# Rotary scores over 128 rows with a zero-padded key, and a forgetting bias built on VectorE from sums broadcast through DRAM

## The chip, the cores and the metric

The kernel runs on one core of one Trainium2 chip. The metric is the device time of one execution in microseconds (us). TensorE (PE in the profile, PEld for its weight loads), VectorE (DVE), ScalarE (ACT) and GpSimd (POOL) each work through an instruction queue of their own in a fixed order; SyncE (SP) and GpSimd issue transfers.

## The reference

Two layers of a transformer trunk on 256 tokens of width 2048, in float32. Each layer normalises and modulates its input, projects it, and runs three attention branches of 8 heads with 128 columns each. The branches' outputs are gated, projected, merged by sigmoid gates and projected once more. The change touches the scores of two branches. Queries are taken in two blocks of 128; the first sees 128 keys, the second 256.

```python
# latent attention: per head 128 plain columns and 64 rotary ones; the rotary key is the same for all heads
k_a = jnp.concatenate([kv_a[..., :MLA_NOPE], k_pe], axis=-1)
s = jnp.einsum('bqhd,bkhd->bhqk', q, k) / math.sqrt(MLA_NOPE + MLA_ROPE)

# forgetting attention: a bias from running sums of log-sigmoids, per head
log_f = jax.nn.log_sigmoid(f_logit + fox_bias)
fcum = jnp.transpose(jnp.cumsum(log_f, axis=1), (0, 2, 1))
s = jnp.einsum('bqhd,bkhd->bhqk', q, k) / math.sqrt(HEAD_DIM)
s = s + fcum[:, :, q0:q0 + n_q, None] - fcum[:, :, None, :n_k]
p = jax.nn.softmax(jnp.where(mask, s, NEG_INF), axis=-1)
```

The third branch, stick-breaking attention, has plain 128-row scores and is not changed.

## The kernel before

**Weight products.** Nearly all of TensorE's time goes into products of activations with weights. Weights come from DRAM in units of 256 rows by up to 1024 columns (`weight_unit`, line 222) into four buffers `raw`. Each unit is split in two halves of 128 rows, and each half into a rounded part `whi` (ScalarE, line 235) and its remainder `wlo` (VectorE, line 237), four buffers each. Three matmuls of 512 columns per pair and output bank follow (lines 281 to 283). So VectorE and ScalarE have to deliver one split half for every 12 matmuls.

**What sets the order.** The program is recorded with a scheduling layer that places each engine's instructions by its own estimate of when they are ready. It sets the attention instructions in between the matmuls of whatever product comes next (mostly the merge gate, `merge_gate`, line 485). On the chip each queue then runs in that order, and a waiting instruction holds up all that stand behind it.

**Latent attention** (line 726). Transposed plain queries and keys lie in `qT` and `kT`, 128 rows a head. The rotary queries of two heads share one 128-row block of `peT`: head 2i in rows 0 to 63, head 2i+1 in rows 64 to 127. The rotary key `kpT` holds the same 64 rows twice, one above the other. `scores` (line 459) does for each query block a plain matmul over 128 rows and adds a rotary one over 64 rows, of the upper or the lower half. In float32 each of these matmuls is a pair of instructions in the trace (x2).

**Forgetting attention** (line 731). The logits `flog` are early results. Line 750 sums them over tokens with a triangle of ones; the sums, plain and negated, are split into rounded and remainder rows (lines 752 to 761). For each head, line 764 selects that head's rows on VectorE, and `biased_scores` (line 468) puts the bias into the score bank by a 256-column matmul (line 472) and adds the plain scores (line 473).

**Softmax** (`attention_head`, line 423). VectorE adds the mask and takes the row maximum in one instruction per query block (line 428), ScalarE does the exponential (line 434), TensorE transposes the result (line 442), ScalarE copies it (line 444), TensorE multiplies with the values (lines 447 to 449), and VectorE scales and gates the output (line 455). Scores, transposes and outputs take turns in two PSUM buffers (`att_tile`).

**Background work.** In both layers weights of the modulation vectors are summed on VectorE (line 300) in between. GpSimd adds them across partitions (line 327) and writes one result to DRAM (line 330), which is broadcast later to all partitions (line 837). In layer 1 this sum across partitions falls just ahead of the forgetting attention (line 723).

Of the kernel before, what the change touches and what calls it, by code (L numbers as in the profile page):

```python
# [9 lines left out]
F32 = mybir.dt.float32  # L10
F32R = mybir.dt.float32r
I32 = mybir.dt.int32
AF = mybir.ActivationFunctionType
ALU = mybir.AluOpType

P = 128
# [26 lines left out]
def trunk(  # L43
# [82 lines left out]
    # quad[:, q] marks rows 32q..32q+7; columns 4 and 5 the last two and the first two such groups  # L126
    quad = const.tile([P, 6], F32, name="quad")
    nc.gpsimd.memset(quad, 0.0)
    for q in range(4):
        nc.gpsimd.memset(quad[32 * q:32 * q + H, q:q + 1], 1.0)  # L130
        nc.gpsimd.memset(quad[32 * q:32 * q + H, 4 + (q < 2):5 + (q < 2)], 1.0)
    sel = const.tile([P, H], F32, name="sel")
    nc.vector.tensor_tensor(out=sel, in0=ident[:, :H], in1=ident[:, 32:32 + H], op=ALU.add)
    for q in (2, 3):
        nc.vector.tensor_tensor(out=sel, in0=sel, in1=ident[:, 32 * q:32 * q + H], op=ALU.add)
# [50 lines left out]
    def rsqrt(v, eps, scale=1.0):  # L186
        """1 / sqrt(scale * v + eps): seed from the exponent bits, three Newton steps."""
# [55 lines left out]
    class Gemm:  # L243
        """out[token, parts' columns] = act^T @ parts, in banks of at most 512 columns."""
# [110 lines left out]
    def normalise_row(src, dst, t, mean):  # L355
        """dst = (src - mean) / sqrt(var + eps) of one token tile; dst is scratch until then."""
# [46 lines left out]
    def rope(src, dst, t, n, eng):  # L403
        """src, dst: [P, n, 2, 32]"""
# [7 lines left out]
    def rms_rows(src, n, t):  # L412
        """src [P, n] in SBUF, scaled in place by its reciprocal root mean square."""
# [8 lines left out]

    def attention_head(S, mask, scale, h, v, g):
        sm = tmp.tile([P, 3 * P], F32, tag="sm", name="sm")
        mx = small.tile([P, 2], F32, tag="mx", name="mx")
        segs = ((0, P), (P, 3 * P))
        for t, (a, b) in enumerate(segs):
            nc.vector.tensor_tensor_reduce(
                out=sm[:, a:b], in0=S[t], in1=mask[:, 2 * P - (b - a):], scale=1.0, scalar=-3.0e38,
                op0=ALU.add, op1=ALU.max, accum_out=mx[:, t:t + 1])  # L430
# [37 lines left out]
    def biased_scores(qT, kT, h, bl, br):  # L468
        S = att_tile()
        for t, n in enumerate((P, 2 * P)):  # L470
            ts_, a = slice(t * P, (t + 1) * P), t * SEQ
            nc.tensor.matmul(S[:, a:a + SEQ], bl[:, ts_], br, start=True, stop=False)
            nc.tensor.matmul(S[:, a:a + n], qT[:, h, ts_], kT[:, h, :n], start=False, stop=True)
        return S[:, :P], S[:, SEQ:]

# [15 lines left out]
    for l in range(DEPTH):  # L491
# [6 lines left out]
        # ================= branch a: latent attention =================  # L498
# [4 lines left out]
        peT = big.tile([P, H // 2 + 1, SEQ], F32, tag="sig", name="peT")  # L503
        qpT, kpT = peT[:, :H // 2], peT[:, H // 2]
# [4 lines left out]
        def evac_a0(t, h, ps):  # L509
# [8 lines left out]
            else:  # L518
# [11 lines left out]
                nc.vector.tensor_copy(out=kpT[:, t * P:(t + 1) * P], in_=tp[:, 2 * P:3 * P])  # L530
# [173 lines left out]
        for n in range(3):  # L704
# [21 lines left out]
            if n == 0:  # L726
                for h in range(H):
                    pb = slice(64 * (h % 2), 64 * (h % 2) + 64)
                    S = scores(qT, kT, h, [(qpT[pb, h // 2], kpT[pb])])
                    attention_head((S[:, :P], S[:, P:3 * P]), m_mla, 1.0 / math.sqrt(HD + ROPE), h, v, g)  # L730
            elif n == 1:
# [7 lines left out]
                # rows 0.., 32.., 64.., 96..: head sums of lf up to a token, twice plain and twice negated  # L739
                lf4 = tmp.tile([P, NT, 4, 32], F32, tag="sm", name="lf4")  # L740
                nc.vector.memset(lf4, 0.0)
                nc.vector.tensor_scalar(
                    lf4[:, :, :2, :H], lf.rearrange("p t (g h) -> p t g h", g=1).broadcast_to([P, NT, 2, H]),
                    root, None, op0=ALU.mult)
                nc.vector.tensor_scalar(
                    lf4[:, :, 2:, :H], lf.rearrange("p t (g h) -> p t g h", g=1).broadcast_to([P, NT, 2, H]),
                    -root, None, op0=ALU.mult)
                ps = att_tile()
                l4 = lf4.rearrange("p t g h -> p t (g h)")
                nc.tensor.matmul(ps[:, :SEQ], l4[:, 0], tri, start=True, stop=False)  # L750
                nc.tensor.matmul(ps[:, P:SEQ], l4[:, 1], tri[:, :P], start=False, stop=True)
                fr = big.tile([P, 4, SEQ], F32R, tag="yhi", name="fr")
                fh, bl = fr[:, 0], fr[:, 1]
                fw = big.tile([P, 3, SEQ], F32, tag="ylo", name="fw")
                fl, base = fw[:, 0], fw[:, 1]
                split(ps[:, :SEQ], fh, fl)
                for dst, q in ((bl, 0), (base, 2)):
# [159 lines left out]
```

## Time and profile before

| | us |
|---|---|
| median of 3 runs | 2192.75 (2189.21 to 2192.93) |
| span of the profiled execution | 2188.8 |
| TensorE busy | 2087.3 (95%) |
| VectorE busy | 1453.2 (66%) |
| ScalarE busy | 985.9 (45%) |
| GpSimd busy | 63.7 (3%) |

For the profiled execution the page gives the span, from its first to its last instruction, and no other time. The median of the runs lies 3.95 us above it, the fastest 0.41 us. The ends of matmuls are modelled and overlap the next one's start, so the pace of TensorE is read from starts: the distance between the starts of two rows.

### The profile page before, as it was taken

Reading aid. Unit: us, or ns where it says so; the run is one execution under the profiler, and the core shown is the slowest. Engines: PE = TensorE matmul, PEld = TensorE weight load, DVE = VectorE, ACT = ScalarE, POOL = GpSimd, SP = SyncE. Lnnn points to the kernel's source line nnn. Section 1 sums busy time; section 2 is a strip of 40 time slices with the busy share of each in tenths; the row PEclk is TensorE's granted clock in tenths of the full one; section 3 lists DMA queues with packets and bytes.
Section 4 is the critical chain, followed back from the end, with each engine's and each line's share of the span. In section 5 each row is a group of like instructions: output and inputs, shape, how many; then the busy total and the mean of one; then the engine's idle time right before and its main releaser. Section 6 shows DMA issues by size and latency. Waiting matters only on the chain.

```text
span 2188.8 us, 24876 instructions
## 1 busy us (share of the span) xinstructions
PE 2087.3 (95%) x9630; PEld 1704.1 (78%) x9630; DVE 1453.2 (66%) x1944; ACT 985.9 (45%) x1259; POOL 63.7 (3%) x80
## 2 busy tenths in 40 slices
PE   4999999999999999999969999999989999999996
PEld 2877878887888878787848878888868888878885
DVE  6898845677558777888586755555575554466466
ACT  4435644343453445634355644444444444464442
POOL 0000000002000020002000000000020000000000
PEclk8999999999999999999979999999999999999998
DMA  8996635787548867786635736666645555555652
GB/s 312 343 333 234 192 116 173 271 300 268 181 152 295 314 257 253 290 323 212 210 135 177 233 121 221 233 221 220 234 160 172 192 183 184 193 190 200 192 204 96
DMA packets 137781, 481.03 MB, mean 220 GB/s; under 512 B 14656, under 2 KB 18880, under 8 KB 127424
## 3 DMA queue, kind: packets, MB, share of 16 engines
q1 hardware_dynamic: 133296, 464.69, 61.3%
q0 software_dynamic: 2080, 14.70, 1.7%
q8 instruction: 75, 1.23, 0.2%
q10 hardware_dynamic: 2288, 0.07, 0.1%
q14 instruction: 42, 0.34, 0.0%
HBM read 475.21 MB, written 4.21 MB: 219 GB/s over the span
## 4 chain that ended last, share of the span: by engine, by line
PE 87%; DVE 8%; ACT 3%; issue 2%; DMA 1%; POOL 0%; DVEq 0%; SPq 0%; POOLq 0%; ACTq 0%
PE acc L282 25%; PE acc L283 25%; PE acc L281 25%; DVE wlo L237 2%; PE att L464 2%; PE acc L620 2%; PE acc L621 2%; PE acc L619 1%; ACT whi L235 1%; PE att L481 1%; PE att L447 1%; PE att L442 1%; PE att L399 1%; DVE wlo L611 1%; DVE cum L782 1%
## 5 line engine op out<-in xcount | busy, mean ns | idle before, releaser
L237 DVE TENSOR_TENSOR wlo<-raw,whi 128x1024 fp32r<-128x1024 f32 (+2 forms) x648 | 813.7, 1261 | 572.9 <-ACT whi L235 572.7
L235 ACT ACTIVATE whi<-raw 128x1024 fp32r<-128x1024 f32 (+2 forms) x648 | 677.6, 1051 | 834.6 <-PE acc L283 782.7
L282 PE MATMUL acc<-wlo,uhi 128*128 128x512 f32 (+1 forms) x1856 | 733.2, 395 | 12.2 <-DVE wlo L237 12.2
L281 PE MATMUL acc<-whi,uhi 128*128 128x512 f32 (+1 forms) x1856 | 727.7, 394 | 4.0 <-ACT whi L235 3.9
L283 PE MATMUL acc<-whi,ulo 128*128 128x512 f32 (+1 forms) x1856 | 727.9, 392 | 0.0
L282 PEld LDWEIGHTS acc<-wlo,uhi 128*128 128x128 f32 x1856 | 351.3, 189 | 82.9 <-DVE wlo L237 14.2
L281 PEld LDWEIGHTS acc<-whi,uhi 128*128 128x128 f32 x1856 | 350.1, 189 | 76.1 <-ACT whi L235 4.3
L283 PEld LDWEIGHTS acc<-whi,ulo 128*128 128x128 f32 x1856 | 350.9, 189 | 68.5 <-issue 1.3
L282 PE MATMUL acc<-wlo,yhi 128*128 128x512 f32 x384 | 149.5, 389 | 2.0 <-DVE wlo L237 2.0
L281 PE MATMUL acc<-whi,yhi 128*128 128x512 f32 x384 | 149.4, 389 | 0.0
L283 PE MATMUL acc<-whi,ylo 128*128 128x512 f32 x384 | 149.4, 389 | 0.0
L300 DVE SCALAR_TENSOR_TENSOR ada_acc<-raw_ada,c_sb,ada_acc 128x2048 f32<-128x2048 f32 x60 | 140.7, 2345 | 0.1
L281 PE MATMUL acc<-whi,mhi 128*128 128x512 f32 x256 | 99.7, 391 | 2.0 <-ACT mhi L201 2.0
L283 PE MATMUL acc<-whi,mlo 128*128 128x512 f32 x256 | 100.5, 392 | 0.0
L282 PE MATMUL acc<-wlo,mhi 128*128 128x512 f32 x256 | 100.0, 391 | 0.0
L327 POOL PARTITION_ALL_REDUCE ada_acc<-ada_acc x4 | 49.9, 12470 | 1296.2 <-DVE ada_acc L300 777.3
L282 PEld LDWEIGHTS acc<-wlo,yhi 128*128 128x128 f32 x384 | 72.1, 188 | 17.4 <-DVE wlo L237 2.5
L281 PEld LDWEIGHTS acc<-whi,yhi 128*128 128x128 f32 x384 | 72.1, 188 | 15.1
L283 PEld LDWEIGHTS acc<-whi,ylo 128*128 128x128 f32 x384 | 72.1, 188 | 14.8
L620 PE MATMUL acc<-wlo,uhi 128*128 128x512 f32 (+1 forms) x192 | 73.8, 386 | 5.6 <-DVE wlo L611 5.4
L619 PE MATMUL acc<-whi,uhi 128*128 128x512 f32 (+1 forms) x192 | 72.4, 385 | 3.5 <-DVE sum_b L625 1.9
L621 PE MATMUL acc<-whi,ulo 128*128 128x512 f32 (+1 forms) x192 | 72.4, 379 | 0.0
(238 smaller groups left out, 1780.8 us busy)
## 6 DMA issues: line engine op xcount, KB each, us to landing
raw<-in_w_in_dram SPq DMA_DIRECT2D x224, 1024.0 KB, 4.9
raw_ada<-in_w_ada_dram SPq DMA_DIRECT2D x64, 1024.0 KB, 4.9
raw<-in_w_branch_dram SPq DMA_DIRECT2D x48, 1024.0 KB, 5.5
raw_s<-in_w_ada_dram SPq DMA_DIRECT2D x64, 512.0 KB, 5.5
raw<-in_w_out_dram SPq DMA_DIRECT2D x32, 1024.0 KB, 5.5
raw_g<-in_w_in_dram SPq DMA_DIRECT2D x16, 1024.0 KB, 6.4
raw<-in_w_in_dram SPq DMA_DIRECT2D x8, 832.0 KB, 4.4
raw<-in_w_uq_dram SPq DMA_DIRECT2D x8, 768.0 KB, 4.5
```

Source lines behind the costliest of these rows:

```text
L235: nc.scalar.activation(hi[:, :width], raw[:, j, :width], AF.Copy)
L237: state["dve"] = nc.vector.tensor_tensor(out=lo[:, :width], in0=raw[:, j, :width], in1=hi[:, :width].bitcast(F32), op=ALU.subtract)
L281: nc.tensor.matmul(ps, ah, hi[:, o:o + w], start=k == 0, stop=False)
L282: nc.tensor.matmul(ps, ah, lo[:, o:o + w], start=False, stop=False)
L283: nc.tensor.matmul(ps, al, hi[:, o:o + w], start=False, stop=k == self.nk - 1)
L300: nc.vector.scalar_tensor_tensor(out=acc, in0=raw, scalar=col, in1=acc, op0=ALU.mult, op1=ALU.add)
L327: nc.gpsimd.partition_all_reduce(acc, acc, P, bass_isa.ReduceOp.add)
L399: nc.tensor.transpose(tp[:, i * P:(i + 1) * P], tm[:, i * P:(i + 1) * P], ident)
L464: nc.tensor.matmul(S[:, a:b], l[:, t * P:(t + 1) * P], r[:, :b - a], start=i == 0, stop=i == len(pairs) - 1)
L619: nc.tensor.matmul(ps, ah, hi, start=j == 0, stop=False)
L620: nc.tensor.matmul(ps, ah, lo, start=False, stop=False)
L621: nc.tensor.matmul(ps, al, hi, start=False, stop=j == 3)
```

## The change

The rotary key is stored twice, once in rows 0 to 63 with zeros below, and once in rows 64 to 127 with zeros above (`kz`). The rotary matmul takes the whole 128-row block of queries of two heads and the key of the right half, so the other head's rows meet zeros. GpSimd fills the zeros once a layer, and VectorE copies the transposed key in two halves.

The forgetting bias no longer goes through matmuls. The sums are formed with tokens on partitions (`fq`), transposed to 8 rows, copied, written to DRAM and read back to all 128 partitions (`fk`, 1 MB), both transfers from GpSimd's queue. For each head VectorE builds `nb` = (sum at the key minus sum at the query) minus mask, two instructions, and the masking instruction of the softmax subtracts it from the scores. The plain scores no longer wait for a bias.

```diff
@@ building blocks
-    def attention_head(S, mask, scale, h, v, g):
-        sm = tmp.tile([P, 3 * P], F32, tag="sm", name="sm")
+    def attention_head(S, masks, scale, h, v, g, sm=None):
+
+        op = ALU.subtract
+        if sm is None:
+            sm, op = tmp.tile([P, 3 * P], F32, tag="sm", name="sm"), ALU.add
...
             nc.vector.tensor_tensor_reduce(
-                out=sm[:, a:b], in0=S[t], in1=mask[:, 2 * P - (b - a):], scale=1.0, scalar=-3.0e38,
-                op0=ALU.add, op1=ALU.max, accum_out=mx[:, t:t + 1])
+                out=sm[:, a:b], in0=S[t], in1=masks[t], scale=1.0, scalar=-3.0e38,
+                op0=op, op1=ALU.max, accum_out=mx[:, t:t + 1])
...
-    def biased_scores(qT, kT, h, bl, br):
-        S = att_tile()
-        for t, n in enumerate((P, 2 * P)):
-            ts_, a = slice(t * P, (t + 1) * P), t * SEQ
-            nc.tensor.matmul(S[:, a:a + SEQ], bl[:, ts_], br, start=True, stop=False)
-            nc.tensor.matmul(S[:, a:a + n], qT[:, h, ts_], kT[:, h, :n], start=False, stop=True)
-        return S[:, :P], S[:, SEQ:]
...
-        peT = big.tile([P, H // 2 + 1, SEQ], F32, tag="sig", name="peT")
-        qpT, kpT = peT[:, :H // 2], peT[:, H // 2]
+        peT = big.tile([P, H // 2 + 2, SEQ], F32, tag="sig", name="peT")
+
+        qpT, kz = peT[:, :H // 2], peT[:, H // 2:]
+        nc.gpsimd.memset(kz[ROPE:, 0], 0.0)
+        nc.gpsimd.memset(kz[:ROPE, 1], 0.0)
...
-                nc.vector.tensor_copy(out=kpT[:, t * P:(t + 1) * P], in_=tp[:, 2 * P:3 * P])
+                for i in range(2):
+                    half = slice(i * ROPE, (i + 1) * ROPE)
+                    nc.vector.tensor_copy(out=kz[half, i, t * P:(t + 1) * P], in_=tp[half, 2 * P:3 * P])
...
                 for h in range(H):
-                    pb = slice(64 * (h % 2), 64 * (h % 2) + 64)
-                    S = scores(qT, kT, h, [(qpT[pb, h // 2], kpT[pb])])
-                    attention_head((S[:, :P], S[:, P:3 * P]), m_mla, 1.0 / math.sqrt(HD + ROPE), h, v, g)
+                    S = scores(qT, kT, h, [(qpT[:, h // 2], kz[:, h % 2])])
+                    attention_head((S[:, :P], S[:, P:3 * P]), (m_mla[:, P:], m_mla), 1.0 / math.sqrt(HD + ROPE), h, v, g)
...
-                lf4 = tmp.tile([P, NT, 4, 32], F32, tag="sm", name="lf4")
...
-                nc.tensor.matmul(ps[:, :SEQ], l4[:, 0], tri, start=True, stop=False)
-                nc.tensor.matmul(ps[:, P:SEQ], l4[:, 1], tri[:, :P], start=False, stop=True)
...
-                split(ps[:, :SEQ], fh, fl)
...
+                nc.vector.tensor_scalar(lf, lf, root, None, op0=ALU.mult)
+
                 ps = att_tile()
+                nc.tensor.matmul(ps[:, :H], tri[:, :P], lf[:, 0], start=True, stop=True)
+                nc.tensor.matmul(ps[:, H:2 * H], tri[:, P:], lf[:, 0], start=True, stop=False)
+                nc.tensor.matmul(ps[:, H:2 * H], tri[:, :P], lf[:, 1], start=False, stop=True)
+                fq = small.tile([P, NT, H], F32, tag="fq", name="fq", bufs=1)
+                nc.vector.tensor_copy(out=fq.rearrange("p t h -> p (t h)"), in_=ps[:, :2 * H])
+                tp = att_tile()
+                for t in range(NT):
+                    nc.tensor.transpose(tp[:H, t * P:(t + 1) * P], fq[:, t], ident)
+                rows = tmp.tile([P, SEQ], F32, tag="um", name="f_rows", bufs=2)[:H]
+                nc.vector.tensor_copy(out=rows, in_=tp[:H, :SEQ])
+                f_dram = dram.tile([1, H * SEQ], F32, name=f"fcum{l}")
+                nc.gpsimd.dma_start(out=f_dram.rearrange("o (h s) -> (o h) s", h=H), in_=rows)
+                fk = big.tile([P, H, SEQ], F32, tag="yhi", name="fk")
+                nc.gpsimd.dma_start(
+                    out=fk.rearrange("p h s -> p (h s)"), in_=f_dram.broadcast_to([P, H * SEQ]))
                 for h in range(H):
-                    br = fr[:, 2 + h % 2]
-                    nc.vector.tensor_scalar(br, base, sel[:, h:h + 1], None, op0=ALU.mult)
-                    attention_head(biased_scores(qT, kT, h, bl, br), m_fox, 1.0 / root, h, v, g)
+
+                    nb = tmp.tile([P, 3 * P], F32, tag="sm", name="sm")
+                    for t, (a, b) in enumerate(((0, P), (P, 3 * P))):
+                        nc.vector.scalar_tensor_tensor(
+                            out=nb[:, a:b], in0=fk[:, h, :b - a], scalar=fq[:, t, h:h + 1],
+                            in1=m_fox[:, 2 * P - (b - a):], op0=ALU.subtract, op1=ALU.subtract)
+                    S = scores(qT, kT, h)
+                    attention_head((S[:, :P], S[:, P:3 * P]), (nb[:, :P], nb[:, P:]), 1.0 / root, h, v, g, nb)
```

The order of latent attention on TensorE stays as it is. Around the forgetting attention the scheduler places things anew. TensorE in layer 0, from the sums to the transposes of the first head, before (`att` is a score or transpose bank, `acc` one of a weight product):

```order
L750 MATMUL att<-tri,lf_4409 128x256
L751 MATMUL att<-tri,lf_4409 128x128
L281 MATMUL acc<-whi,uhi 128x512
...
L472 MATMUL att<-fr 128x256
L473 MATMUL att<-kT,qT 128x128
L472 MATMUL att<-fr 128x256
L473 MATMUL att<-kT,qT 128x256
L282 MATMUL acc<-wlo,uhi 128x512
...
L442 MATMUL att<-ident,sm 128x128
```

There are 28 matmuls of the weight product between the sums and the first scores, and 9 between the scores and the first transpose. The same place now:

```order
L731 MATMUL att<-lf,tri 128x8
L732 MATMUL att<-lf,tri 128x8
L733 MATMUL att<-lf,tri 128x8
L271 MATMUL acc<-whi,uhi 128x512
L272 MATMUL acc<-wlo,uhi 128x512
L738 MATMUL att<-ident,fq 8x128 x2
L457 MATMUL att<-kT,qT 128x128
L457 MATMUL att<-kT,qT 128x256
L273 MATMUL acc<-whi,ulo 128x512
...
L435 MATMUL att<-ident,sm 128x128
```

The first scores stand two matmuls behind the sums, and 53 matmuls of the weight product follow before the first transpose. In layer 1 the counts are 42 and 8 before, and 3 and 53 now.

VectorE in layer 0 at the same place, before (`g` is the gate's last piece, `fw` and `fr` the split sums, `ISA sm,mx` the masking):

```order
L392 SCALAR_TENSOR_TENSOR g<-th,acc 128x512
L202 SCALAR_TENSOR_TENSOR fw<-att,fr 128x256
L237 TENSOR_TENSOR wlo<-raw,whi 128x1024
L758 TENSOR_SCALAR fw<-fw,quad 128x256
L760 SCALAR_TENSOR_TENSOR fr<-fr,quad,fw 128x256
L237 TENSOR_TENSOR wlo<-raw,whi 128x1024
L758 TENSOR_SCALAR fw<-fw,quad 128x256
L760 SCALAR_TENSOR_TENSOR fw<-fr,quad,fw 128x256
L764 TENSOR_SCALAR fr<-fw,sel 128x256 x2
L237 TENSOR_TENSOR wlo<-raw,whi 128x1024
L428 ISA sm,mx<-att,m_fox 128x128
```

And now:

```order
L735 COPY fq<-att 128x16
L227 TENSOR_TENSOR wlo<-raw,whi 128x1024
L382 SCALAR_TENSOR_TENSOR g<-th,acc 128x512
L740 COPY f_rows<-att 8x256
L227 TENSOR_TENSOR wlo<-raw,whi 128x1024 x3
L750 SCALAR_TENSOR_TENSOR sm<-fk,fq,m_fox 128x128
L750 SCALAR_TENSOR_TENSOR sm<-fk,fq,m_fox 128x256
L421 ISA sm,mx<-att,sm 128x128
```

The copy of the sums stands in front of a weight remainder, and the first build, which needs the broadcast, behind three remainders. In layer 1 there are six of them.

GpSimd in layer 1, around the sum across partitions, before:

```order
L327 ISA ada_acc<-ada_acc 128x2048
L330 DMA gate_11925<-ada_acc 16x1x128
L842 DMA lg<-in_ln_g_dram 128x2048
L844 DMA lb<-in_ln_b_dram 128x2048
L837 DMA gate<-gate_11925 128x2048
```

And now:

```order
L317 ISA ada_acc<-ada_acc 128x2048
L320 DMA gate_11912<-ada_acc 16x1x128
L742 DMA fcum_11931<-f_rows 8x256
L744 DMA fk<-fcum_11931 128x2048
L831 DMA lg<-in_ln_g_dram 128x2048
```

Both new transfers stand behind the sum across partitions and the write of its result.

## Rows read from the trace of the kernel before

**Rows 1.** The page: busy engines, and the chain that ended last by engine.

```profile
PE 2087.3 (95%) x9630; PEld 1704.1 (78%) x9630; DVE 1453.2 (66%) x1944; ACT 985.9 (45%) x1259; POOL 63.7 (3%) x80
...
PE 87%; DVE 8%; ACT 3%; issue 2%; DMA 1%; POOL 0%; DVEq 0%; SPq 0%; POOLq 0%; ACTq 0%
```

**Rows 2.** TensorE in order of time, one rotary head, layer 0: start, us, instruction.

```profile
284.37 0.39 PE L449 MATMUL att<-v,pt 128*128 128x128 f32 x2
284.59 0.39 PE L464 MATMUL att<-kT,qT 128*128 128x128 f32 x2
284.90 0.49 PE L464 MATMUL att<-peT 64*128 64x128 f32 x2
285.32 0.70 PE L464 MATMUL att<-kT,qT 128*128 128x256 f32 x2
...
286.57 0.50 PE L282 MATMUL acc<-wlo,uhi 128*128 128x512 f32 x1
286.91 0.39 PE L283 MATMUL acc<-whi,ulo 128*128 128x512 f32 x1
```

**Rows 3.** The same view, two stick-breaking heads' scores, layer 0.

```profile
862.67 1.47 PE L464 MATMUL att<-kT,qT 128*128 128x128 f32 x8
863.79 0.58 PE L281 MATMUL acc<-whi,uhi 128*128 128x512 f32 x1
```

**Rows 4.** Line 464: what its idle time ended with, us and times.

```profile
  issue: 5.3, 16
```

**Rows 5.** TensorE in order of time, forgetting attention, layer 0.

```profile
575.40 0.59 PE L750 MATMUL att<-tri,lf 128*128 128x256 f32 x2
...
575.97 0.48 PE L281 MATMUL acc<-whi,uhi 128*128 128x512 f32 x1
...
582.19 0.39 PE L281 MATMUL acc<-whi,uhi 128*128 128x512 f32 x1
...
588.13 0.39 PE L449 MATMUL att<-v,pt 128*128 128x128 f32 x2
...
589.06 0.59 PE L283 MATMUL acc<-whi,ulo 128*128 128x512 f32 x1
589.48 0.40 PE L281 MATMUL acc<-whi,uhi 128*128 128x512 f32 x1
```

**Rows 6.** DMA issues: tile, queue, count, size, median us to landing.

```profile
lb<-in_ln_b_dram POOLq DMA_DIRECT2D x2, 1024.0 KB, 9.1
gate<-gate POOLq DMA_DIRECT2D x2, 1024.0 KB, 4.9
...
gate<-ada_acc POOLq DMA_DIRECT2D x2, 8.0 KB, 3.6
```

**Rows 7.** VectorE in order of time, forgetting attention, layer 0.

```profile
577.15 0.68 DVE L392 SCALAR_TENSOR_TENSOR g<-th,acc 128x512 f32<-128x512 f32 x1
...
581.67 0.48 DVE L760 SCALAR_TENSOR_TENSOR fw<-fr,quad,fw 128x256 f32<-128x256 f32 x1
```

**Rows 8.** VectorE in order of time, layer 1, ahead of its forgetting attention.

```profile
1589.49 8.66 DVE L237 TENSOR_TENSOR wlo<-raw,whi 128x1024 fp32r<-128x1024 f32 x1
...
1609.41 1.22 DVE L237 TENSOR_TENSOR wlo<-raw,whi 128x1024 fp32r<-128x1024 f32 x1 [0.97 <-ACT whi L235]
```

**Rows 9.** GpSimd there.

```profile
1587.95 11.87 POOL L327 PARTITION_ALL_REDUCE ada_acc<-ada_acc  x1 [462.67 <-DVE ada_acc L300]
```

**Rows 10.** TensorE there.

```profile
1598.20 0.80 PE L282 MATMUL acc<-wlo,uhi 128*128 128x512 f32 x1 [7.36 <-DVE wlo L237]
...
1612.15 0.29 PE L442 MATMUL att<-ident,sm 128*128 128x128 f32 x1
```

**Rows 11.** Stretches: us, busy time of each engine, granted clock, DMA share, GB/s.

```profile
575.00:635.00 60.00, 59.89 (x319) 48.61 (x318) 38.28 (x99) 30.44 (x63) 0.00 (x0) 1.00 0.41 135
912.00:922.00 10.00, 10.00 (x56) 7.97 (x55) 8.82 (x12) 5.25 (x8) 1.05 (x2) 1.00 0.90 310
1598.00:1604.00 6.00, 5.80 (x15) 4.55 (x16) 6.00 (x10) 1.06 (x1) 2.34 (x2) 0.54 0.44 141
```

More of the change, by code (lines that the diff above doesn't have):

```diff
@@ L125, in trunk @@
     nc.gpsimd.memset(m_mla[0:64, P + 64:], NEG)
[L127 to L135, printed above, removed]
     rst = const.tile([P, 3 * P], F32, name="rst")
@@ L738, in trunk @@
                     out=lf, in0=flog, scalar=0.0, in1=lf, op0=ALU.min, op1=ALU.subtract)
-                lf4 = tmp.tile([P, NT, 4, 32], F32, tag="sm", name="lf4")
[L741 to L747, printed above, removed]
@@ L748, in trunk @@
-                ps = att_tile()
-                l4 = lf4.rearrange("p t g h -> p t (g h)")
-                nc.tensor.matmul(ps[:, :SEQ], l4[:, 0], tri, start=True, stop=False)
-                nc.tensor.matmul(ps[:, P:SEQ], l4[:, 1], tri[:, :P], start=False, stop=True)
[L752 to L755, printed above, removed]
@@ L756, in trunk @@
-                split(ps[:, :SEQ], fh, fl)
-                for dst, q in ((bl, 0), (base, 2)):
-                    nc.vector.tensor_scalar(
-                        fw[:, 2], fl, quad[:, q + 1:q + 2], quad[:, 4 + q // 2:5 + q // 2], op0=ALU.mult, op1=ALU.add)
-                    nc.vector.scalar_tensor_tensor(
-                        out=dst, in0=fh.bitcast(F32), scalar=quad[:, q:q + 1], in1=fw[:, 2], op0=ALU.mult, op1=ALU.add)
-                for h in range(H):
-                    br = fr[:, 2 + h % 2]
-                    nc.vector.tensor_scalar(br, base, sel[:, h:h + 1], None, op0=ALU.mult)
-                    attention_head(biased_scores(qT, kT, h, bl, br), m_fox, 1.0 / root, h, v, g)
+                nc.vector.tensor_scalar(lf, lf, root, None, op0=ALU.mult)
```

## The prediction

> **What bounds the kernel now.** I read the page first. TensorE is busy for 95% of the span and carries 87% of the chain that ended last; VectorE has 66% and 8% [rows 1]. So an edit is worth what it takes from TensorE's queue, and one that lengthens VectorE's work costs something only where TensorE then waits. Next I read TensorE in order of time through the three attention stages. None runs alone: a head's scores, transposes and value products stand between the matmuls of a weight product, which follow one another every 0.23 us (27 steps from 575.97 to 582.19 [rows 5]). The head's chain through VectorE and ScalarE is covered by those matmuls.
>
> In the rotary stage the covering stops. The pair before a head's scores takes 0.22 us (284.37 to 284.59), the first score pair 0.31, the 64-row rotary pair 0.42 for the same 128 columns, the two 256-column pairs 1.25 together, and the next matmul begins at 286.57 [rows 2]. The weight loads show idle time that no instruction ends, 16 times, once a head [rows 4]. Four 128-row pairs of the same sizes, in the stick-breaking stage, take 1.12 us from the first to the matmul behind them [rows 3], against 1.98 here. The excess sits where the row count changes from 128 to 64 and back, four times a head.
>
> Last I read the forgetting stage on all engines, since the new path there runs over GpSimd's queue: how long its transfers take [rows 6], and what GpSimd, VectorE and TensorE do ahead of it in layer 1 [rows 8 to 10].
>
> **Rotary scores.** The matmuls stay in number and place; the second operand becomes 128 rows tall, half of them zero. Before: from the first score to the second matmul behind the group, 284.59 to 286.91, 2.32 us. After, by the 128-row rows: 1.12 for the group [rows 3], then 0.42 for the first matmul after it, as it is after 128-row scores (589.06 to 589.48 [rows 5]): 1.54. That is 0.78 a head, 16 heads: 12.5 us. Bounds: nothing, if the rotary pair is slow for another reason; at most 1.10 a head (17.6 us), if all four pairs went at 0.22 and the matmul behind at 0.34 as now. I take the rows with the same shapes. TensorE gets to the transposes sooner, but the chain to them starts when the last score is done, and both move together. The added work is small: two 64-row copies for one 128-row copy, four times, on a VectorE with idle time, and four fills on GpSimd; its queue holds those of layer 1 in front of the load of the residual rows, which waits for a later stage. I cost these at nothing; uncovered, they would be about 1 us.
>
> **Forgetting scores.** Each head loses two 256-column bias matmuls. Before: 588.13 (the pair in front) to 589.48 is 1.35 us [rows 5]. After: 0.22 for that pair, 0.56 for a 128 and a 256 score pair (half of rows 3), 0.42 behind: 1.20. That is 0.15 a head and 2.4 us over 16; bounds 0 and 0.46 a head (7.4 us), if the pairs went at 0.22 and the following matmul at 0.23. VectorE loses one 256-column multiply a head and gains a 128- and a 256-column build, at 0.3 and 0.48 us by the nearest two-input form [rows 7]: some 0.4 us a head more, 3.5 us in a stage of 60 where it is busy for 38 [rows 11]. It stays covered as long as a head takes TensorE over 5 us.
>
> **The sums.** In layer 0 the two products with the triangle took 0.57 us of TensorE (575.40 to 575.97). Now three narrow pairs (0.22 each, the weight load's pace), two transposes (about 0.2) and a short wait for the copy between them make some 0.96: plus 0.4. In layer 1 all this, and the first scores, fall into the 7.36 us for which TensorE waits for a weight remainder that VectorE finishes only after 8.66 us, while GpSimd sums across partitions [rows 8 to 10]: nothing.
>
> **The new wait.** The first build waits for the broadcast `fk`, behind it on VectorE's queue stand all of that head's softmax, the next builds and the weight remainders; on TensorE the transposes of the first head wait, and everything behind them. The order now puts 53 ordinary matmuls between the first scores and these transposes in each layer. Layer 0: 575.40 + 0.66 + 2 x 0.23 + 0.3 + 0.56 + 0.19 + 53 x 0.23 = 589.8 is when TensorE is there. The gate's last multiply now ends near 578.1 (577.15 + 0.68, and about 0.2 for the copy ahead of it), the copy of the rows near 578.6. The 8 KB write takes 3.6 and the 1 MB broadcast 4.9, the same shape from a DRAM row as the gate's [rows 6]: 587.1. Two builds (0.78), the next head's build in between (0.3), and 1.52 from the masking to the transposes (1610.63, the end of the remainder in front of it [rows 8], to 1612.15 [rows 10]) give 589.7. That is even; with some scatter I take 0.5 us. Its ends are 0 and, if the broadcast takes the 9.1 of `lb`, 4.1.
>
> Layer 1: GpSimd is free at 1599.82, the gate's write goes out first, then the sums near 1600.7; landed 1604.3, broadcast 1609.2. VectorE's order has six remainders ahead of the build, the last of which ends near 1610.63 [rows 8], so the broadcast is not the last to come. Ready: 1610.63 + 2.6 = 1613.2. TensorE is there at 1612.15 + 6 x 0.23 (56 matmuls for 50) - 0.9 (the scores that moved ahead) = 1612.6. Wait 0.6; with 9.1, 3.4.
>
> **Sum.** -12.5 - 2.4 + 0.4 + 0.5 + 0.6 = -13.4 us. The page gives the profiled execution's span alone, 2188.8 us; the runs' median is 3.95 above it. The span would be 2175.4 and the median 2179.4.
>
> **Rivals.** *The broadcast is late.* At 9.1 in both layers the waits are 7.5 in place of 1.1: 6.4 back, 2185.8. For it: the loads of `lb` from this queue had that as their median, and weights stream beside it. Against: the gate's took 4.9 twice, with a DMA share of 0.90 at the first; in this stage the share is 0.41 [rows 11].
>
> *The zero rows buy nothing.* Then only the forgetting stage is left, -0.9: 2191.9. The trace speaks against it with 0.42 against 0.22 for equal columns, and the idle weight loads. "TensorE: Matmul & The Clock Gate" of the Trainium skill (Why this matters for your kernels) says that a matmul over 32 rows takes as long as one over 128, and that the gain of short ones is running at once in different rows of the array. By that rule padding saves nothing and may lose an overlap; but no two rotary pairs here stand together in different halves, so the overlap is not there to lose. "TensorEngine Tiling (Array Packing)" (Key Properties) says that a change of tiling mode drains TensorE, which is what rows 2 look like; by it the 12.5 stands.
>
> *More than that*, by the upper bounds: -17.6 - 7.4 + 1.5 = -23.5, 2169; nothing in the trace has 256 columns at 0.22.
>
> *Slower: the round trip through DRAM stalls VectorE.* One late transfer isn't enough: the waits must pass 14.5 us together. If the write and the broadcast both take 9.1, `fk` lands 5.5 later again in each layer: 11 more, and a wait of some 9 us in layer 0 lowers the granted clock as the one in layer 1 does (0.54 over 6 us [rows 11], about 2.5 us of pace). That gives -7.0 + 11 + 2.5 = +6.5, 2199. For it: VectorE was held for 8.66 us while GpSimd worked [rows 8, 9], so the two do get in each other's way. Against: 3.6 for the same 8 KB. "SBUF — State Buffer" (SBUF: two separate sides) states that VectorE with two SBUF inputs and a GpSimd instruction that reads SBUF lock each other out, and (A bandwidth-pool intuition that's wrong) that GpSimd can't write a DMA's descriptors while VectorE holds the shared port. By that the new builds and the remainders beside them would delay both transfers.
>
> **How the numbers follow.** Forecast 0.70; late broadcast 0.11; nothing from the zero rows 0.06; more 0.07; slower 0.06. The range, 2173 to 2188, reaches half way to the upper bounds on one side and past the late broadcast on the other, and leaves out the other two. A measurement of this kernel can tell some 0.2% (4.4 us) from no change, so under 2188.4 is faster: 0.70 + 0.11 + 0.07 less 0.02 for part of the late case, 0.86; same 0.08; slower 0.06.
>
> **What would show it.** Right: score groups of the rotary stage near 1.1 us with the 128-row rotary pair at the pace of its neighbours; no bias matmuls; the weight loads' unexplained idle time gone; TensorE waiting less than about 2 us ahead of the first forgetting transposes in each layer. Wrong: rotary groups still near 2 us, or VectorE waiting for `fk` for several microseconds with TensorE waiting behind it, or a granted clock under 1 there in layer 0.

## The result, and the profile after

| | before | after |
|---|---|---|
| median of the runs, us | 2191.72 (4 runs, 2189.21 to 2192.93) | 2176.78 (4 runs, 2176.1 to 2180.91) |
| span of the profiled execution, us | 2188.8 | 2175.2 |

The ratio of the changed kernel's time to that of before is 0.9936, with a 95% interval of 0.9922 to 0.995. The forecast was 2179.4 us, with a range of 2173 to 2188, and a span shorter by 13.4 us; it is shorter by 13.6. Five more executions of the changed kernel beside eleven of before gave 2179.1 against 2192.3 us: 0.9943, 0.9931 to 0.9955. The scatter goes with TensorE's clock: of 23 executions of before, those with a mean granted clock of 0.986 took 2188.6 to 2189.9 us, and those with 0.984 or 0.985 took 2190.7 to 2193.7.

The page of the changed kernel, busy engines and the chain that ended last:

```profile
PE 2071.8 (95%) x9606; PEld 1700.4 (78%) x9606; DVE 1455.5 (67%) x1951; ACT 984.4 (45%) x1257; POOL 66.5 (3%) x79
...
PE 24%; DVE 2%; ACT 1%; DMA 0%; issue 0%; DVEq 0%
```

TensorE is busy for 15.5 us less than in [rows 1], VectorE for 2.3 us more. The chain now reaches back a quarter of the span only: it is followed to the broadcast `fk` of layer 1, for which VectorE waited at 1599 us, and ends there. Line numbers are those of the changed kernel: 457 the scores, 435 the transposes of the softmax, 742 and 744 the two transfers through DRAM, 750 the new builds.

**A rotary head** on TensorE in order of time (start, us, instruction), layer 0:

```profile
283.17 0.39 PE L442 MATMUL att<-v,pt 128*128 128x128 f32 x2
283.39 0.39 PE L457 MATMUL att<-kT,qT 128*128 128x128 f32 x2
283.62 0.39 PE L457 MATMUL att<-peT 128*128 128x128 f32 x2
283.84 0.60 PE L457 MATMUL att<-kT,qT 128*128 128x256 f32 x2
...
284.52 0.58 PE L272 MATMUL acc<-wlo,uhi 128*128 128x512 f32 x1
284.94 0.39 PE L273 MATMUL acc<-whi,ulo 128*128 128x512 f32 x1
```

The rotary pair has 128 rows and moves at its neighbours' pace: 0.22 us to the next start where it was 0.42 [rows 2]. From the first score to the second matmul behind the group it is 284.94 - 283.39 = 1.55 us, for 2.32 before. With the pair in front it is 1.77 for 2.54 us, and all 16 heads agree within 0.05 us. Line 457 has no idle time that no instruction ends, where line 464 had it 16 times [rows 4].

**A forgetting head** in the same view:

```profile
584.75 0.39 PE L442 MATMUL att<-v,pt 128*128 128x128 f32 x2
584.98 0.82 PE L457 MATMUL att<-kT,qT 128*128 128x128 f32 x4
585.45 0.58 PE L271 MATMUL acc<-whi,uhi 128*128 128x512 f32 x1
585.86 0.39 PE L272 MATMUL acc<-wlo,uhi 128*128 128x512 f32 x1
```

From the pair in front to the second matmul behind it is 1.11 us, for 1.35 before [rows 5].

**The new path.** The DMA issues (size, median us to landing), then GpSimd, VectorE and TensorE in order of time; a bracket is idle time and what ended it:

```profile
fk<-fcum POOLq DMA_DIRECT2D x2, 1024.0 KB, 6.7
fcum<-f_rows POOLq DMA_DIRECT2D x2, 8.0 KB, 3.2
```

```profile
570.51 0.53 POOL L742 DMA_DIRECT2D fcum<-f_rows  x1 [30.39 <-DVE f_rows L740]
572.69 0.60 POOL L744 DMA_DIRECT2D fk<-fcum  x1 [1.65 <-DMA fcum<-f_rows]
...
1575.68 11.87 POOL L317 PARTITION_ALL_REDUCE ada_acc<-ada_acc  x1 [457.31 <-DVE ada_acc L290]
...
1588.35 0.53 POOL L742 DMA_DIRECT2D fcum<-f_rows  x1
1593.72 0.58 POOL L744 DMA_DIRECT2D fk<-fcum  x1 [4.85 <-DMA fcum<-f_rows]
```

```profile
580.38 0.75 DVE L750 SCALAR_TENSOR_TENSOR sm<-fk,fq,m_fox 128x128 f32<-128x128 f32 x2 [3.60 <-DMA fk<-fcum]
...
1577.69 8.19 DVE L227 TENSOR_TENSOR wlo<-raw,whi 128x1024 fp32r<-128x1024 f32 x1
...
1599.48 0.75 DVE L750 SCALAR_TENSOR_TENSOR sm<-fk,fq,m_fox 128x128 f32<-128x128 f32 x2 [1.56 <-DMA fk<-fcum]
```

```profile
582.60 0.33 PE L435 MATMUL att<-ident,sm 128*128 128x128 f32 x1 [1.16 <-ACT sm L427]
...
588.92 0.33 PE L435 MATMUL att<-ident,sm 128*128 128x128 f32 x1 [0.37 <-ACT sm L427]
...
1585.93 0.79 PE L272 MATMUL acc<-wlo,uhi 128*128 128x512 f32 x1 [6.47 <-DVE wlo L227]
...
1601.70 0.33 PE L435 MATMUL att<-ident,sm 128*128 128x128 f32 x1 [1.66 <-ACT sm L427]
```

In layer 0 the 8 KB write is through 2.2 us after its issue, and the broadcast 7.7 us after its own (572.69 to 580.38, where VectorE starts); VectorE waits 3.60 us for it, and TensorE 1.16 us at the first masked head and 0.37 at the second. In layer 1 the write goes out at 1588.35, behind the sum across partitions (1575.68, 11.87 us) and the gate's transfer; the broadcast goes out at 1593.72, 5.4 us behind the write. VectorE waits 1.56 us for it at 1599.48, TensorE 1.66. The remainder beside the sum across partitions still takes VectorE 8.19 us [rows 8, 9], but TensorE waits for it 6.47 us where it waited 7.36 [rows 10]: the sums and the first scores are done before.

**The clock.** The 5 us behind the first and behind the second wait beside the sum across partitions in layer 0, before, then after (us, busy time of each engine, granted clock, DMA share, GB/s):

```profile
543.92:548.92 5.00, 5.00 (x15) 3.96 (x16) 3.35 (x4) 1.06 (x1) 2.47 (x2) 0.66 0.80 277
805.60:810.60 5.00, 5.00 (x22) 4.11 (x23) 4.39 (x4) 1.06 (x1) 1.63 (x1) 1.00 0.80 272
```

```profile
537.34:542.34 5.00, 5.00 (x22) 4.11 (x23) 4.39 (x4) 1.06 (x1) 2.47 (x2) 1.00 0.80 283
797.14:802.14 5.00, 5.00 (x15) 3.97 (x16) 3.35 (x3) 0.94 (x1) 1.62 (x1) 0.66 0.79 279
```

Both kernels wait 2.80 us ahead of the first of these stretches and 2.04 us ahead of the second, for the same weight remainders. Before, the clock behind the first wait was 0.66 (a mix of the levels 1.2 and 2.4 GHz over these 5 us) and behind the second 1; after, it was 1 and then 0.66. So 1.7 us (5.00 x 0.34) were lost at the one place before, and as much at the other after; neither kernel gained by it. Without a look at the clock column, the ledger below would show a gain between two points where the code is the same.

**The ledger.** Starts on TensorE where all kernels begin the same piece of work: before, and what the others are earlier (-) or later than that, in us; the last three are experiments, below.

| piece | before | after | rotary alone | forgetting alone | order of pairs |
|---|---|---|---|---|---|
| first rotary scores, L0 | 278.07 | -0.49 | +2.70 | +3.08 | +2.96 |
| end of the first wait beside the sum, L0 | 543.92 | -6.58 | -3.30 | +3.06 | +0.10 |
| forgetting sums, L0 | 575.40 | -8.19 | -3.33 | +1.40 | +0.05 |
| end of the second wait, L0 | 805.60 | -8.46 | -3.32 | -0.44 | +0.06 |
| first stick-breaking scores, L0 | 862.67 | -6.89 | -3.37 | -0.46 | +0.06 |
| first rotary scores, L1 | 1253.11 | -6.07 | -2.87 | -0.37 | -0.17 |
| forgetting sums, L1 | 1589.10 | -12.27 | -8.98 | -0.42 | -3.15 |
| first stick-breaking scores, L1 | 1927.27 | -13.63 | -9.61 | -2.72 | -3.52 |
| span | 2188.8 | -13.6 | -9.6 | -2.7 | -3.5 |

The first row lies ahead of everything that was changed. The three that start some 3 us late have a granted clock of 0.66 to 0.75 in the 5 us from 220 or 225 us, where the other two have 1, and were already 1.4 to 2.0 us late at 72 us. What an edit is worth is the difference between two rows. The rotary heads give 6.09 us in layer 0 (-0.49 to -6.58) and 6.20 in layer 1 (-6.07 to -12.27). The forgetting stage gives 0.27 in layer 0 (-8.19 to -8.46) and 1.36 in layer 1 (-12.27 to -13.63). Of the 1.36 some 0.5 us is the clock: over the 8 us behind the wait beside the sum across partitions it was 0.67 before and 0.73 after (not shown).

### The profile page after: what moved, and what is told of

It is laid out like the page before. It is cut to its first block, busy times and chain, and to the rows that moved or that the text cites. A ratio compares the mean times of both kernels' runs of the same rounds, so it can differ in the third digit from the quotient of the medians.

```text
span 2175.2 us, 24840 instructions
## 1 busy us (share of the span) xinstructions
PE 2071.8 (95%) x9606; PEld 1700.4 (78%) x9606; DVE 1455.5 (67%) x1951; ACT 984.4 (45%) x1257; POOL 66.5 (3%) x79
## 5 line engine op out<-in xcount | busy, mean ns | idle before, releaser
L273 PE MATMUL acc<-whi,ulo 128*128 128x512 f32 (+1 forms) x1856 | 727.9, 392 | 0.0
L600 ACT ACTIVATE whi<-raw_g 128x1024 fp32r<-128x1024 f32 (+1 forms) x48 | 46.3, 1002 | 59.1 <-DMA raw_g<-in_w_in_dram 53.9
```

Of the source, the lines that this page charges most:

```text
L273: nc.tensor.matmul(ps, al, hi[:, o:o + w], start=False, stop=k == self.nk - 1)
L600: nc.scalar.activation(hi, raw[:, 2 * j:2 * j + 2, :w], AF.Copy)
```

## Experiments

The theory to be tested was that of the prediction: the gain is a price per rotary head which sits in the changes of the row count, the forgetting part is worth little, and of the waits the broadcast decides.

**The rotary key alone**, and **the forgetting part alone**. The first is the kernel before with the `kz` lines of the diff, the second the changed kernel with these lines undone:

```
-        qpT, kz = peT[:, :H // 2], peT[:, H // 2:]
+        qpT, kpT = peT[:, :H // 2], peT[:, H // 2]
...
-                    S = scores(qT, kT, h, [(qpT[:, h // 2], kz[:, h % 2])])
+                    pb = slice(64 * (h % 2), 64 * (h % 2) + 64)
+                    S = scores(qT, kT, h, [(qpT[pb, h // 2], kpT[pb])])
```

> The kernel before with the padded rotary key alone; the forgetting branch keeps its four-row bias matmuls. My theory: the gain is a price of each rotary head, 0.78 us x 16 = 12.5 us, so 2191.7 - 12.5 = 2179.2 us, and the first head's score group takes 1.13 us + 0.42 us on TensorE as in the changed kernel. Rival A (the zero rows buy nothing and the forgetting part carries it): 2191.7 us. Rival B (the marks of the changed kernel lie: -6.1 us in each rotary branch is in part the clock): somewhere between, with the L0 rotary branch less than 6 us shorter.

> The changed kernel with the 64-row rotary key put back; the forgetting bias comes through DRAM. My theory: 16 heads save 0.15 us each on TensorE (-2.4), the sums cost +0.4 in L0, the waits for the first masked scores 1.5 us (L0, 1.16 + 0.37) and 1.7 us (L1), and the wait beside the all-reduce shrinks by 0.9 us: about +0.3 us on the sum of the marks to -1.7 us, so 2190 to 2192 us, no difference that can be told. Rival (the broadcast wait is the larger, the rotary part gains more than the total): slower than before by over 4 us. Rival (the forgetting part gives half of the 14.9 us): 2184 us.

Beside 23 runs of before at 2191.49 us, the rotary key alone took 2180.95 us (5 runs; ratio 0.9959, 0.9948 to 0.9971), and the forgetting part alone 2188.13 (12 runs; 0.9987, 0.9977 to 0.9996). By the ledger the rotary heads give 6.00 and 6.11 us, 0.76 a head: my theory, and the zero rows are what buys it. (The medians differ by 10.5 us only; the profiled execution was 2.70 us behind before any rotary head.) The forgetting part alone gives 1.84 us in layer 0 and 2.30 in layer 1, more than I expected, and more than the 0.27 and 1.36 that it gives in the changed kernel. The difference is the waits. This is TensorE at the first masked head of layer 0, in the kernel with the forgetting part alone:

```profile
590.99 0.33 PE L435 MATMUL att<-ident,sm 128*128 128x128 f32 x1
```

There is no idle time in front of it, with the same 53 matmuls of cover. The broadcast took 5.3 us here (583.11 to 588.41), for 7.7 in the changed kernel. In layer 1 TensorE waits 0.20 us at its first masked head, for 1.66; with the 0.5 us of the clock taken off, that is the difference there.

**The order of a head's pairs.** One line of the kernel before:

```
-            for i, (l, r) in enumerate(pairs):
+            for i, (l, r) in enumerate(pairs[::-1] if t else pairs):
```

> The kernel before with one line changed: in a rotary head's second segment the 64-row pair is issued ahead of the 128-row pair, so that the row count changes twice a head where it changed four times; the same matmuls of the same shapes. Theory 'the price is in changing the row count': half of it goes, 0.39 us x 16 = -6.2 us, 2185.5 us. Rival 'a 64-row pair is slow in itself': 2191.7 us, no change. Between them, the part that goes is the part of the changes.

2186.28 us (11 runs; 0.9977, 0.9968 to 0.9985): -5.2 us. TensorE, one head, in order of time:

```profile
286.99 0.39 PE L449 MATMUL att<-v,pt 128*128 128x128 f32 x2
287.21 0.39 PE L464 MATMUL att<-kT,qT 128*128 128x128 f32 x2
287.53 0.92 PE L464 MATMUL att<-peT 64*128 64x128 f32 x4
...
289.14 0.39 PE L283 MATMUL acc<-whi,ulo 128*128 128x512 f32 x1
```

The two 64-row pairs stand together, and from the pair in front (286.99) to the second matmul behind (289.14) it is 2.15 us. Before it was 2.54 (284.37 to 286.91 [rows 2]), in the changed kernel 1.77 (283.17 to 284.94). The ledger has 2.86 and 2.98 us a layer, about half of the padding's gain, for no change but an order.

**Only 64 rows.** Half of the plain pair is left out, so that all four pairs of a head read the same 64 rows:

```
-        pairs = [(qT[:, h], kT[:, h])] + list(more)
+        lo = slice(ROPE * (h % 2), ROPE * (h % 2) + ROPE) if more else slice(0, P)
+        pairs = [(qT[lo, h], kT[lo, h])] + list(more)
```

> The kernel before with half of the rotary heads' 128-row pair left out (rows 64 to 127 for even heads, 0 to 63 for odd ones, so the scores are not the reference's): all four pairs of a head read the same 64 rows and nothing changes the row count within a head. Theory 'the price is in changing the row count, at 0.2 us each': the group of a head's pairs takes what the changed kernel's 128-row pairs take, 1.1 us to the start of the last pair where before took 1.6 to 2.0, and the changes left are the one on entering and the one on leaving a head. Rival 'a 64-row pair has a price of its own': the group takes longer than before, over 2 us. By the first, 2191.5 - 6 = 2185.5 us; by the second, 2191.5 + 6 = 2197.5 us.

One run, 2184.05 us. TensorE, one head:

```profile
283.97 0.39 PE L449 MATMUL att<-v,pt 128*128 128x128 f32 x2
284.29 0.48 PE L465 MATMUL att<-kT,qT 64*128 64x128 f32 x2
284.62 0.38 PE L465 MATMUL att<-peT 64*128 64x128 f32 x2
284.84 0.59 PE L465 MATMUL att<-kT,qT 64*128 64x256 f32 x2
285.27 0.59 PE L465 MATMUL att<-peT 64*128 64x256 f32 x2
...
286.13 0.39 PE L283 MATMUL acc<-whi,ulo 128*128 128x512 f32 x1
```

Within the head a 64-row pair takes 0.22 us for 128 columns (284.62 to 284.84) and 0.43 for 256 (284.84 to 285.27), just what 128 rows take. Time is lost on entering the head from the 128-row pair in front, where the first pair starts late (0.32 us for 0.22) and takes 0.33, and on leaving it, where it is 0.86 us from the last pair to the second matmul behind (285.27 to 286.13), for 0.67 in the changed kernel (not shown). From the pair in front to the second matmul behind: 2.16 us. So with four changes of the row count a head takes 2.54, with two of them 2.15 or 2.16, with none 1.77: 0.19 us a change, in either arrangement. The rival of slow 64-row pairs falls. Both operands of a matmul change their rows together here, so which of them costs the time is not shown.

**The sums early.** The gate's logarithm goes to the start of the branch, the sums and both transfers behind the first of its four projections:

```
+                    if n == 1 and dst is qT:
+                        ps = att_tile()
+                        nc.tensor.matmul(ps[:, :H], tri[:, :P], lf[:, 0], start=True, stop=True)
...
+                        nc.gpsimd.dma_start(
+                            out=fk.rearrange("p h s -> p (h s)"), in_=f_dram.broadcast_to([P, H * SEQ]))
```

> The changed kernel with the logarithm of the forget gate taken at the start of the forgetting branch, and its sums, transposes and the two DMAs through DRAM behind the first of that branch's projections, 100 us ahead of their use. Theory 'TensorE's new waits at the first masked heads are the broadcast's': 1.16 + 0.37 us in L0 and 1.66 us in L1 go, 2176.8 - 3.2 = 2173.6 us, and no instruction of VectorE waits for fk. Rival 'the wait is VectorE's backlog, the broadcast only came last': under 1 us gained, 2176 us. Rival 'the masks that run earlier take the cover from the all-reduce in L1': slower than the changed kernel.

> The variant with the sums behind the branch's first projection once more, to be set beside the changed kernel's nine runs (2176.1 to 2181.4 us, median 2178.8). Theory 'it is worth its waits less the larger wait beside the all-reduce, 1 to 2 us, the rest is the clock': 2177.5 us. Rival 'no gain': 2178.8 us.

> The changed kernel with the forgetting sums, transposes and the two DMAs through DRAM behind the third of the branch's four projections, 40 us ahead of use, where the variant that put them behind the first gained nothing: its trace had no wait for fk, but lost 3.6 us more to TensorE's lower clock level (10.7 us against 7.1 us, each stretch's busy time times one minus its granted clock) and the wait beside the all-reduce in L1 was 7.4 us again. Theory 'the clock took it, and where its sags fall moves with the code': no wait for fk, 2176.8 - 3.2 + 0.9 = 2174.5 us, if the mean clock is 0.985 as in the changed kernel. Rival 'any kernel without the wait for fk loses as much to the clock': 0.983 again and 2177 us.

TensorE at the first masked head of layer 0 and beside the sum across partitions in layer 1, sums behind the first projection:

```profile
578.85 0.33 PE L435 MATMUL att<-ident,sm 128*128 128x128 f32 x1
...
1588.63 0.80 PE L272 MATMUL acc<-wlo,uhi 128*128 128x512 f32 x1 [7.37 <-DVE wlo L227]
```

The wait for the masks is gone in both layers, and the other one is at 7.37 us again, as before the change [rows 10], since no sums stand in front of it now. Yet the medians are 2177.58 and, once more, 2178.18 us (5 runs each), and behind the third projection 2179.36 (6 runs, 2175.5 to 2185.89). The changed kernel's nine runs have 2178.82 as their median. At an equal mean clock the early sums are worth about 1 us: at 0.985 two runs at 2175.5 and 2175.6, against 2176.1 to 2176.9 for three of the changed kernel; at 0.983 2176.8 to 2179.4 (five runs) against 2178.8 to 2179.2 (three). That is less than can be told. What the clock takes (from 60 us on, the busy time of each 5 us times one minus its clock) moved from 10.7 us in one profile of this variant to 7.6 in the other, so the first expectation's rivals can't be told apart by the medians; the waits did what the theory said.

**The broadcast in two.** Head 0's part goes first, the other seven behind it; then the same with an 8-column copy on GpSimd between the two, which holds the second back until the first has landed:

```
+                nc.gpsimd.dma_start(out=f0, in_=f_dram[:, :SEQ].broadcast_to([P, SEQ]))
+                nc.gpsimd.tensor_copy(out=fk[:, 1, :8], in_=f0[:, :8])
+                nc.gpsimd.dma_start(
+                    out=fk[:, 1:].rearrange("p h s -> p (h s)"),
+                    in_=f_dram[:, SEQ:].broadcast_to([P, (H - 1) * SEQ]))
```

(The second line is the second variant's alone.)

> The changed kernel with the broadcast in two: head 0's 128 KB first, by itself, then the other seven heads' 896 KB. In the order of instructions TensorE's first masked transposes now stand behind 41 projection matmuls (9.3 us at 0.227) from the first masked scores, where they stand behind 53 (12.0 us). Theory 'the wait is the megabyte's bytes': the small broadcast lands some 2 to 3 us after its issue, the mask of head 0 is built before TensorE is through its 41 matmuls, the waits of 1.16 + 0.37 and 1.66 us go: 2176.8 - 3.2 = 2173.6 us. Rival 'most of the 5.7 us from issue to landing is there for any size': the first mask starts when it did, the cover is 2.7 us shorter in each layer, 2176.8 + 5.4 = 2182 us.

> The changed kernel itself once more, as the measure for the variants beside it. Expected: 2176.8 us, mean clock 0.985, waits of 1.2 us (L0) and 1.7 us (L1) for the first masked scores; if its clock comes out lower, the time is higher by 2.2 us for each 0.001.

The split took 2184.0 us, beside 2179.1 for the changed kernel on the same chip. In the latter's profile TensorE's waits for the masks were

```profile
PE att L435 <- ACT sm L427: 1.7, 3, 0.7
```

that is 0.70 and 0.37 in layer 0 and 0.62 in layer 1, for a broadcast of 6.2 us in place of 6.7. Part of the shorter wait in layer 1 is no gain: over the 8 us behind the wait beside the sum across partitions the clock was 0.63, for 0.73 in the first profile (not shown), so TensorE came to the masks some 0.8 us later. The split: GpSimd, VectorE, TensorE, and the stretch that follows.

```profile
576.36 0.62 POOL L745 DMA_DIRECT2D f<-fcum  x1 [1.39 <-DMA fcum<-f_rows]
576.97 0.54 POOL L746 DMA_DIRECT2D fk<-fcum  x1
```

```profile
582.60 0.75 DVE L753 SCALAR_TENSOR_TENSOR sm<-f,fq,m_fox 128x128 f32<-128x128 f32 x2 [4.62 <-DMA f<-fcum]
```

```profile
585.70 0.48 PE L435 MATMUL att<-ident,sm 128*128 128x128 f32 x1 [3.06 <-ACT sm L427]
```

```profile
585.70:590.70 5.00, 5.00 (x22) 4.22 (x23) 3.39 (x14) 1.99 (x4) 0.00 (x0) 0.70 0.66 213
```

The 128 KB were there 6.2 us after their issue (576.36 to 582.60), with 2.7 us less cover TensorE waited 3.06 us, and in the 5 us behind that wait the clock was 0.70, where it is 1 in the changed kernel. In layer 1 it was a wait of 2.44 us, and 0.66 behind it. So the split cost what the rival said, but partly by the clock, which neither had. Whether those 6.2 us were the small transfer's own was open; the copy between the two tells.

> The split variant (head 0's 128 KB first, 41 matmuls of cover) with the other 896 KB held back on GpSimd until the small broadcast has landed, by an 8-column copy between them. Theory 'the small broadcast was slow because the large one shared the engines with it': alone it lands in 3 to 3.5 us, as the 8 KB write does, TensorE's first waits of 3.06 and 2.44 us fall to under 0.5 us, and the granted clock behind them stays at 1; head 1's mask may then wait for the 896 KB, some 1 us: 2184.0 - 5 - 3 + 2 = 2178 us. Rival 'a broadcast to 128 rows takes some 5 us at any size': the first waits stay near 3 and 2.4 us, head 1's mask waits on top, 2184 us or more.

```profile
576.17 0.62 POOL L745 DMA_DIRECT2D f<-fcum  x1 [1.39 <-DMA fcum<-f_rows]
580.43 0.19 POOL L746 COPY fk<-f 128x8 f32<-128x8 f32 x1 [3.64 <-DMA f<-fcum]
580.92 0.54 POOL L747 DMA_DIRECT2D fk<-fcum  x1 [0.30 <-POOL fk L746]
```

```profile
583.51 0.33 PE L435 MATMUL att<-ident,sm 128*128 128x128 f32 x1 [1.05 <-ACT sm L427]
...
1598.90 0.33 PE L435 MATMUL att<-ident,sm 128*128 128x128 f32 x1 [0.65 <-ACT sm L427]
...
1606.75 0.33 PE L435 MATMUL att<-ident,sm 128*128 128x128 f32 x1 [2.22 <-ACT sm L427]
```

Alone, the 128 KB were there after 4.3 us in layer 0 (576.17 to 580.43) and 3.4 in layer 1, the waits fell to 1.05 and 0.65 us, and the granted clock behind them stayed at 1. So in layer 0 the large broadcast beside it had cost the small one 1.9 of its 6.2 us, and the wait fell by 2.0. In layer 1 the small one came only 0.5 us sooner (3.9 in the split), but the wait fell by 1.8. These are the 8 us behind the wait beside the sum across partitions there, in the split, then here:

```profile
1591.90:1599.90 8.00, 8.00 (x28) 6.46 (x29) 5.78 (x7) 2.12 (x2) 3.09 (x4) 0.77 0.60 218
```

```profile
1586.01:1594.01 8.00, 8.00 (x23) 6.30 (x24) 5.50 (x6) 1.28 (x2) 3.12 (x4) 0.62 0.61 219
```

With the clock at 0.62 for 0.77, TensorE came to the masks 1.2 us later (8.00 x 0.15) through the same 41 matmuls, and so waited less without being any faster. The price of the order is paid later: the 896 KB leave 4 us later, and in layer 1 the second head's transposes wait 2.22 us. 2178.51 us (4 runs): no gain over one transfer.

**The broadcast twice**, into the same tile:

```
-                nc.gpsimd.dma_start(
-                    out=fk.rearrange("p h s -> p (h s)"), in_=f_dram.broadcast_to([P, H * SEQ]))
+                for _ in range(2):
+                    nc.gpsimd.dma_start(
+                        out=fk.rearrange("p h s -> p (h s)"), in_=f_dram.broadcast_to([P, H * SEQ]))
```

> The changed kernel with the 1 MB broadcast sent twice into the same tile, the second after the first has landed. In the order of instructions TensorE's first masked transposes now stand behind 72 (L0) and 77 (L1) projection matmuls from the first masked scores, where the changed kernel has 53: 4.3 and 5.4 us more cover at 0.227 us. Theory 'the wait is the landing of fk less the cover': fk lands 5.7 to 6.7 us later by the changed kernel's own broadcasts, so TensorE's waits of 1.1 (with the second) and 0.6 us, in the changed kernel's second profile, become 2.5 to 3.5 us and 0.9 to 1.9 us, and as the 3.06 us wait of the split variant did, one near 3 us costs some 1.5 us of lower clock: 2179 + 2.5 + 1.5 = 2183 us. Rival 'the cover hides any broadcast': the waits stay, 2179 us.

One run, 2192.42 us, span 2190.7. TensorE at the first masked head of each layer, and the stretch behind the first:

```profile
594.04 0.47 PE L435 MATMUL att<-ident,sm 128*128 128x128 f32 x1 [4.34 <-ACT sm L427]
...
1618.34 0.33 PE L435 MATMUL att<-ident,sm 128*128 128x128 f32 x1 [3.77 <-ACT sm L427]
```

```profile
594.04:599.04 5.00, 5.00 (x18) 4.39 (x19) 3.67 (x8) 1.85 (x4) 0.00 (x0) 0.50 0.09 10
```

The four broadcasts took 7.3, 7.9, 5.0 and 8.1 us. TensorE waits 9.1 us in all at the masks, against 1.7 in the control: +7.4. What the clock takes, summed as above, is 14.1 us for 8.0: +6.1, of which 4.2 lie in the two stretches of 5 us behind these waits (0.50 and 0.66). Together 13.5 of the 15.3 us between the two spans; the rest is open. The theory had the direction and the clock, but its waits were too small, as its broadcasts were. By this one run, a wait of this length is paid in full, and again by the clock.

## Why the prediction was right, step by step

- **Rotary scores, 0.78 us a head: right.** 0.77 by the rows of one head, 0.76 by the ledger of the rotary key alone. The place was right too: in the changes of the row count, 0.19 us each, four a head, 64 changes in 16 heads. Of the two rules of the Trainium skill that the prediction weighed, both fit and don't contradict each other here. Fewer rows take as long as more, as "TensorE: Matmul & The Clock Gate" (Why this matters for your kernels) says of 32: the trace agrees for 64, with 0.22 and 0.43 us. A change of tiling drains the engine, as "TensorEngine Tiling (Array Packing)" (Key Properties) says: the trace agrees in that each change costs, 0.19 us; that a drain is what takes it no run here shows.
- **Forgetting scores, 0.15 us a head: too small.** It measured 0.24, so 3.8 us for 2.4. I took half of the eight-instruction row [rows 3], 0.56 us, for two score pairs; two pairs by themselves take 0.47 (584.98 to the matmul behind, at 585.45).
- **The sums in layer 0, +0.4: right.** From their first matmul (567.21) to the first scores (568.57) it is 1.36 us with two projection matmuls of 0.23 in between, so 0.90, for 0.57 before.
- **The sums in layer 1 fall into a wait: right, but not credited.** The wait fell by 0.9 us, 7.36 to 6.47. I used this only to bring TensorE to the next wait earlier, and left it out of the sum.
- **The new waits, 0.5 and 0.6 us: too small in the first profile**, 1.53 and 1.66; in the control 1.07 and 0.62, the latter with the help of a lower clock ahead of it. The step that failed is the broadcast at 4.9 us, taken from the gate's [rows 6]. It took 5.4 to 7.7 us in these two profiles, which is between the two rows that I had, and nearer to `lb`'s 9.1 than I put it. In layer 1 I had said that VectorE's remainders would end later than the broadcast; VectorE waited 1.56 us for it. There the write failed too: with 5.4 us from its issue to the broadcast's, for 3.6, it made up 1.8 of the 2.6 us by which `fk` was later than I had it (5.8 for 4.9 is the rest). Why the transfers took longer, by the weights streaming beside them or by VectorE's work, no run here separates.

With the measured sizes the sum is -12.3 - 3.8 + 0.3 - 0.9 + 1.5 + 1.7 = -13.5 us. That the total was so near is luck: the underpriced scores and the missing 0.9 happen to stand against the underpriced waits. The late broadcast (2185.8) had the right mechanism at less than half of its price: 3.2 us of waits for 7.5. The slower rival's way of going wrong is real: the doubled broadcast has a 4.34 us wait in layer 0 and a clock of 0.50 behind it, and comes out at 2192.4. In the changed kernel's own profiles the largest wait at the masks is 1.66 us; 2.44 is the smallest one there that had a lower clock behind it.

No version beat the changed kernel by more than can be told.

## What to carry to other kernels

Before shortening an operand, look at its neighbours: on this kernel a short pair saved nothing, and each change of the row count cost 0.19 us; padding with zeros, or only setting equal shapes side by side, takes that back. A round trip through DRAM costs TensorE no wait as long as the order puts enough other work in front of its first reader; judge that cover by the slowest transfer of that size in the trace, not by the fastest. When two profiles are compared piece by piece, read the granted clock of each stretch first, since 1.7 us came and went between points with the same code.

## What the runs showed of the hardware that was not expected

- The same wait of 2.80 us was followed by a clock of 0.66 over 5 us in one profile and of 1 in another; that of 2.04 us by 1 in one and 0.66 in the other. At the masks, waits of 2.22 us and less had 1 behind them, those of 2.44, 3.06, 3.77 and 4.34 had 0.66, 0.70, 0.66 and 0.50. So the length of a wait alone doesn't decide; what does stays open.
- A lower clock ahead of a wait hides in it: with the clock at 0.62 for 0.77 over 8 us, TensorE came 1.2 us later and waited so much less.
- A 128 KB broadcast from one DRAM row took 3.4 to 4.3 us by itself until its first reader started, and 3.9 to 6.2 with 896 KB issued right behind it on the same queue (the lower figures in layer 1). 1 MB took 4.7 to 8.4 us from issue to landing over all variants. So an eighth of the bytes still took more than half of the time that the whole took in the same place (4.3 for 7.2 to 7.7 us in layer 0, 3.4 for 5.4 to 5.8 in layer 1).
